# Earlier splits of the rows of O^T and another order of the additions and weights between attention and the feed-forward part of a two-layer trunk

## The chip, the cores and the metric

The kernel runs on one core of one Trainium2 chip. The metric is device time in microseconds (us) of one execution. PE is TensorE, DVE VectorE, ACT ScalarE, POOL GpSimd, and SP SyncE, which issues nearly all DMAs here.

## What is computed

```python
def reference(x, mem, ...):                      # x is 1024 tokens x 1024, two layers
    h = x
    for layer in range(2):
        xn, mn = rmsnorm(h, norm_mix[layer]), rmsnorm(mem, norm_mem[layer])
        proj = xn @ (w_in_fox if layer == 0 else w_in_dil)[0]
        mix = fox_attention(...) if layer == 0 else dilated_attention(...)   # 12 heads of 64
        heads = concat([mix, memory_attention(qm, mn, w_mem_kv[layer])])     # 4 more heads
        h = h + merge_heads(heads) @ w_out[layer]
        h = h + conv_ffn(rmsnorm(h, norm_ffn[layer]), w_up[layer], ...)
    return rmsnorm(h, norm_final)
```

## The kernel before

All values are held transposed, features on partitions and tokens along the free dimension, and the 1024 tokens are worked on as two halves of 512. A float32 product is made of three matmuls: each operand is split into a high part, which is a cast, and a low part, which is the operand less its high part. So a group for one block of 128 input features is high by high (L175), high weights by low input (L176) and low weights by high input (L177). `load_w` fetches a piece of weights of 128x512 by a DMA on SP (L121, four buffers `wraw`), casts it on ACT (L122, `whi`) and subtracts on POOL (L123, `wlo`). A pair `whi`, `wlo` holds two pieces, 128x1024, the weights of one output row, and there are three such pairs.

**Attention.** There are six pairs of heads (`pair` 0 to 5), and in each two heads with eight blocks of queries. `fill` holds generators of matmuls, the projections of the next pairs among them, which are mixed with the blocks' scores (L514, L515), transposes (L531) and products with v (L851) at due times given as numbers (L799 to L808). The softmax of a block runs on DVE (maximum L518, scaling L525) and ACT (exponential L522). Each transposed block is cast on ACT (L532, `pth`) and subtracted on DVE (L533, `ptl`). A projection of k is cast on ACT (L492), subtracted on POOL (L494, `kla`, `klb`) and then moved to other partitions by DMAs on SP (L103). The order on PE follows the program. ACT, DVE, POOL and SP take their instructions in the order that the framework's scheduler makes of it.

**Rows of O^T.** The output of each pair of heads is a row of O^T, 128 features by 1024 tokens. Two more rows come from the memory heads. All rows but that of the last pair are written to DRAM (`o_scr`, L547) and read back, one half at a time, by `load_o`: a DMA on SP (L296), a cast on ACT (L297, `xh`) and a subtraction on POOL (L298, `xl`). The raw row lies in a ring of five buffers (`sqt`), which other short-lived tiles share. The order of the rows (`KORD`) is 0, 1, 2, 3, 6, 7, 4, 5. Row 5 never leaves the chip (`fold`, L543). The tiles `xh` and `xl` of a half are those that held the input of the projections of that half.

**Output projection.** It has eight rows of outputs. `out_part(0, 6)` and `out_part(1, 4)` are generators in `fill` (L807, L808) that multiply the first seven rows of O^T with six rows of outputs of half 0 and four of half 1. Each loads its seven rows of O^T at its start (L604). What is left is done by `out_rest` (L309): the rest of a row that `out_part` began (kind "f", one group, weights `wol`) and whole rows (kind "c", eight groups). Behind each row come the residual's addition on DVE (L302), a store (L329), a square on ACT (L331) and the addition of the square to `acc` on DVE (L333). For half 0 this runs at the end of attention (`out_last`). For half 1 it is `rest_1` (L1066), with the order c4, f0, f1, c5, f2, f3, c6, c7.

**Start of the feed-forward part.** From L1076 on the order on PE, ACT, DVE and POOL is that of the code. `next(rest_1)` issues one row of the above, and `x0` prepares the first three inputs of the up-projection from half 0. The up-projection of a pair of feature blocks `j` takes seven products (`product(j, m, bank)`, four groups each) of sums of weights and sums of inputs. The sums of weights are made by `w_alpha` (an addition on DVE, L944, into a tile `asum`), `w_beta` (none) and `w_delta` (two subtractions, L958). Each is split by a cast on ACT (L972) and a subtraction on POOL (L975). `norm_stages` sums the squares of half 1 over features with matmuls (L136), takes the inverse root on POOL (L140), spreads it on DVE (L142), and broadcasts it by a matmul (L146) when it is next resumed. From the broadcast `rb` the inputs of half 1 are scaled on DVE (L378), cast (L371) and subtracted (L374). product(0,5) is the first one to use them.

## Time and profile before

| what | value |
|---|---|
| median of 3 runs | 2610.03 us (2608.42 to 2611.66) |
| the profiled execution | 2601.88 us, of which the span is 2600.1 us |
| mean granted clock of TensorE in it | 0.983 of full |
| PE busy | 2433.2 us (94%) |
| DVE busy | 1585.9 us (61%) |
| POOL busy | 1244.7 us (48%) |
| ACT busy | 1211.6 us (47%) |

The profile comes from one execution, on a time axis that starts with the span. Busy time is that of instructions on an engine, and issue of DMAs is not counted in it. Matmuls overlap their neighbours, so a busy PE isn't PE at its peak: what is to be read are the stretches in which it idles, the instruction that ended each, and the clock that was granted.

### The profile page before, as it was taken

To read this page: it belongs to the slowest core of one execution; us is meant where nothing else is said; L and a number is where in the kernel's file an instruction comes from. 1 tells how busy PE (TensorE), PEld (TensorE's weight loads), DVE (VectorE), ACT (ScalarE), POOL (GpSimd) and SP (SyncE) were. 2 spreads that over 40 slices of the span, in tenths; PEclk is the share of its full clock that TensorE was granted. 3 is DMA by queue.
4 is the path that set the end of the run, shared out by engine and by line. 5 is a ranking of instruction groups with operands and counts; after the bars stand their busy time and mean duration, and the time that the engine had idled before them with its cause. 6 is when DMAs were issued, how large, how long until landed. Compare 5 with 4: busy or idle time off the path is not lost.

```text
span 2600.1 us, 34495 instructions
## 1 busy us (share of the span) xinstructions
PE 2433.2 (94%) x12274; PEld 2023.5 (78%) x12274; DVE 1585.9 (61%) x2777; ACT 1211.6 (47%) x2192; POOL 1244.7 (48%) x797
## 2 busy tenths in 40 slices
PE   5899999898899999999998899988889999999997
PEld 5778888676688888888877797876767888887886
DVE  6667677667866666523156767675777666665322
ACT  6555555543444443533345555555434434444321
POOL 4332323354566666556453333335436666664543
PEclk9999999999999999999999999999999999999999
DMA  5122222441322222654332222234412222237432
GB/s 175 50 76 58 74 60 88 140 155 52 106 73 93 78 89 90 228 180 145 117 124 60 72 57 68 57 100 152 142 61 81 90 81 73 95 125 237 133 128 77
DMA packets 143829, 269.06 MB, mean 103 GB/s; under 512 B 18716, under 2 KB 23452, under 8 KB 143656
## 3 DMA queue, kind: packets, MB, share of 16 engines
q1 hardware_dynamic: 142792, 266.16, 31.7%
q8 instruction: 96, 1.57, 0.3%
q10 hardware_dynamic: 864, 0.69, 0.1%
q14 instruction: 77, 0.63, 0.1%
HBM read 198.58 MB, written 47.24 MB: 95 GB/s over the span
## 4 chain that ended last, share of the span: by engine, by line
PE 72%; DVE 9%; issue 8%; POOL 4%; ACT 4%; DMA 3%; SPq 0%; POOLq 0%; DVEq 0%; ACTq 0%
PE PS L175 16%; PE PS L176 16%; PE PS L177 16%; PE PS L851 3%; PE PS L531 3%; PE PS L1358 3%; PE PS L1359 3%; PE PS L1360 3%; POOL wlo L123 2%; PE PS L1312 2%; PE PS L1310 2%; PE PS L1311 2%; DVE y L525 1%; DMA graw<-gscr 1%; PE PS L515 1%
## 5 line engine op out<-in xcount | busy, mean ns | idle before, releaser
L123 POOL TENSOR_TENSOR wlo<-wraw,whi 128x512 fp32r<-128x512 f32 x354 | 466.6, 1339 | 621.9 <-ACT whi L122 506.5
L175 PE MATMUL PS<-t,ahi 128*128 128x512 f32 x1056 | 413.8, 392 | 7.5 <-DVE cv L1034 6.7
L176 PE MATMUL PS<-t,ahi 128*128 128x512 f32 x1056 | 413.6, 392 | 4.8 <-DVE t L374 4.8
L177 PE MATMUL PS<-t,alo 128*128 128x512 f32 x1056 | 412.6, 391 | 0.0
L175 PE MATMUL PS<-xh,whi 128*128 128x512 f32 x704 | 307.8, 437 | 24.4 <-ACT whi L122 10.4
L122 ACT CAST whi<-wraw 128x512 fp32r<-128x512 f32 x354 | 201.4, 607 | 242.7 <-issue 67.8
L176 PE MATMUL PS<-xl,whi 128*128 128x512 f32 x704 | 284.5, 404 | 13.2 <-POOL xl L298 13.2
L177 PE MATMUL PS<-xh,wlo 128*128 128x512 f32 x704 | 284.3, 404 | 6.9 <-POOL wlo L123 6.8
L1030 ACT ACTIVATE cv<-PS,cw 128x1024 f32<-128x1024 f32 x88 | 106.2, 1207 | 322.0 <-DVE PS L1011 315.2
L175 PEld LDWEIGHTS PS<-t,ahi 128*128 128x128 f32 x1056 | 198.7, 188 | 54.0 <-issue 9.3
L176 PEld LDWEIGHTS PS<-t,ahi 128*128 128x128 f32 x1056 | 198.6, 188 | 49.3 <-DVE t L374 7.0
L177 PEld LDWEIGHTS PS<-t,alo 128*128 128x128 f32 x1056 | 198.6, 188 | 41.8
L1034 DVE SCALAR_TENSOR_TENSOR cv<-PS,cw,cv 128x1023 f32<-128x1023 f32 (+1 forms) x176 | 221.7, 1278 | 7.4 <-ACT cv L1030 4.3
L975 POOL TENSOR_TENSOR alo<-araw,ahi 128x1024 fp32r<-128x1024 f32 x88 | 212.2, 2413 | 4.4 <-ACT ahi L972 4.4
L522 ACT ACTIVATE y<-y,m 128x128 f32<-128x128 f32 (+1 forms) x192 | 149.2, 778 | 122.4 <-DVE m L518 120.1
L533 DVE TENSOR_TENSOR ptl<-PS,pth 128x512 fp32r<-128x512 f32 (+3 forms) x288 | 152.0, 551 | 56.9 <-ACT pth L532 55.7
L532 ACT CAST pth<-PS 128x512 fp32r<-128x512 f32 (+3 forms) x288 | 129.8, 478 | 101.8 <-PE PS L531 97.9
L175 PEld LDWEIGHTS PS<-xh,whi 128*128 128x128 f32 x704 | 138.4, 197 | 46.3 <-ACT whi L122 13.2
L177 PEld LDWEIGHTS PS<-xh,wlo 128*128 128x128 f32 x704 | 136.4, 194 | 40.7 <-POOL wlo L123 11.1
L176 PEld LDWEIGHTS PS<-xl,whi 128*128 128x128 f32 x704 | 137.7, 196 | 37.0 <-POOL xl L298 21.4
L302 DVE TENSOR_TENSOR h<-h,PS 128x512 f32<-128x512 f32 x56 | 37.7, 685 | 203.3 <-PE PS L1360 165.3
L1281 DVE TENSOR_TENSOR g<-graw,g 128x512 fp32r<-128x512 f32 x88 | 80.2, 942 | 118.8 <-ACT g L1280 118.5
(218 smaller groups left out, 5815.6 us busy)
## 6 DMA issues: line engine op xcount, KB each, us to landing
araw<-in_wu SPq DMA_DIRECT2D x176, 256.0 KB, 3.6
wraw<-in_wd SPq DMA_DIRECT2D x168, 256.0 KB, 3.0
gscr<-cv SPq DMA_DIRECT2D x44, 512.0 KB, 2.6
graw<-gscr SPq DMA_DIRECT2D x88, 256.0 KB, 3.7
wraw<-in_wo SPq DMA_DIRECT2D x64, 256.0 KB, 2.8
wraw<-in_wq SPq DMA_DIRECT2D x56, 256.0 KB, 2.9
hfscr<-h SPq DMA_DIRECT2D x32, 256.0 KB, 2.1
h<-hfscr SPq DMA_DIRECT2D x32, 256.0 KB, 4.0
```

The costliest lines, as they stand in the source:

```text
L122: nc.scalar.copy(hi[:, w], raw[:, :n])
L123: nc.gpsimd.tensor_tensor(lo[:, w], raw[:, :n], hi[:, w].bitcast(F32), op=ALU.subtract)
L175: nc.tensor.matmul(ps, lhsT=whi(k), rhs=xhi(k), start=(first and k == 0), stop=False)
L176: nc.tensor.matmul(ps, lhsT=whi(k), rhs=xlo(k), start=False, stop=False)
L177: nc.tensor.matmul(ps, lhsT=wlo(k), rhs=xhi(k), start=False, stop=(last and k == nk - 1))
L522: nc.scalar.activation(y[:, :nk], y[:, :nk], AF.Exp, bias=m[:, npc - 1:npc], scale=-1.0, accum_out=m[:, 2:3])
L532: nc.scalar.copy(ph, tp[:, :nj, :])
L533: nc.vector.tensor_tensor(pl, tp[:, :nj, :], ph.bitcast(F32), op=ALU.subtract)
L975: eng.tensor_tensor(o[2], o[0], o[1].bitcast(F32), op=ALU.subtract)
L1030: nc.scalar.activation(t, u, AF.Identity, bias=w(3), scale=w(2))
L1034: V.scalar_tensor_tensor(t[:, d:], u[:, :T - d], w(2 - d), t[:, d:], op0=ALU.mult, op1=ALU.add)
L1281: nc.vector.tensor_tensor(t[:, 1, :], raw, t[:, 0, :].bitcast(F32), op=ALU.subtract)
```

## The change

It has four pieces. `load_o` can now load some of its rows and go on later, and six rows of half 0 are loaded by a new generator `o_first`, which stands in `fill` ahead of the last projection of k for half 1 (`pair_k(5, 1)`) and behind that for half 0. The seventh row, row 4, is still loaded at the start of `out_part(0, 6)`. Six rows of half 1 are loaded when `out_part(0, 6)` comes to its third row of outputs. `out_rest` loads the weights of the second whole row before its first row, and those of whole row m+2 behind the matmuls of whole row m, which held the same buffers. At the start of the feed-forward part, residual and square additions of `rest_1` go ahead of `w_alpha(1)` and `w_delta(1)`, `asum` of j = 1 lies in another ring, and the norm's first stage and its broadcast each stand one product later.

```diff
@@ -286,16 +286,20 @@
     def load_h(l, n, half, dst=None):
         nc.sync.dma_start((dst or H[half])(n), a["xT"][:, n, half * HT:half * HT + HT] if l == 0 else h_scr[n][half])
 
-    def load_o(l, half):
-
-        if (l, half) in O:
-            return O[l, half]
-        oh, ol = O[l, half] = x_tiles(half)
-        for c in KORD[:-1]:
+    DONE = {}
+
+    def load_o(l, half, n=NPAIR + 1):
+
+        if (l, half) not in O:
+            O[l, half] = x_tiles(half)
+            DONE[l, half] = 0
+        oh, ol = O[l, half]
+        for c in KORD[DONE[l, half]:n]:
             raw = sqt("oraw")
             nc.sync.dma_start(raw, o_scr[l][c][:, half * HT:half * HT + HT])
             nc.scalar.copy(oh[:, c, :], raw)
             nc.gpsimd.tensor_tensor(ol[:, c, :], raw, oh[:, c, :].bitcast(F32), op=ALU.subtract)
+        DONE[l, half] = max(n, DONE[l, half])
         return oh, ol
 
     def residual(ps, n, half, src=None):
@@ -313,18 +317,19 @@
         whole = [n for kind, n in order if kind == "c"]
         ws = {whole[0]: load_w(a["wo"][l, whole[0]])}
         wl = load_w(a["wol"][l])
+        ws[whole[1]] = load_w(a["wo"][l, whole[1]])
         yield
         for i, (kind, n) in enumerate(order):
             if kind == "f":
                 hi, lo, ks = *wl, [(NPAIR - 1, n)]
             else:
-                m = whole.index(n) + 1
-                if m < len(whole):
-                    ws[whole[m]] = load_w(a["wo"][l, whole[m]])
                 hi, lo, ks = *ws.pop(n), [(c, c) for c in KORD]
             ps = psum()
             mm3(ps, lambda k: cols(hi)(ks[k][1]), lambda k: cols(lo)(ks[k][1]),
                 lambda k: oh[:, ks[k][0], :], lambda k: ol[:, ks[k][0], :], len(ks))
+            m = whole.index(n) + 2 if kind == "c" else len(whole)
+            if m < len(whole):
+                ws[whole[m]] = load_w(a["wo"][l, whole[m]])
             residual(ps, n, half, PART[l] if half and kind == "f" else None)
             nc.sync.dma_start(hf_scr[l][n][half], H[half](n))
             sq = acc if i == 0 else sqt("sq")
@@ -611,11 +616,17 @@
                 for n in range(rows if half else KD):
                     load_h(l, n, half, dst)
                 for n in range(rows):
+                    if half == 0 and n == 2:
+                        load_o(l, 1, NPAIR)
                     hi, lo = load_w(a["wo"][l, n])
                     ps = psp()
                     yield from mm3g(ps, lambda k: cols(hi)(KORD[k]), lambda k: cols(lo)(KORD[k]),
                                     lambda k: oh[:, KORD[k], :], lambda k: ol[:, KORD[k], :], KD - 1, 216)
                     nc.vector.tensor_tensor(dst(n), dst(n), ps, op=ALU.add)
+
+            def o_first():
+                load_o(l, 0, NPAIR)
+                yield 0
 
 
             def out_last():
@@ -801,6 +812,8 @@
                 if v:
                     fill.add(v[0], V, 16 * p - 6, 16 * p - 13, ("va", p))
                 fill.add(pair_k(p, 0), QK, 16 * p - (1.5, 2.5)[l], 16 * p - 8, ("a", p))
+                if p == NPAIR - 1:
+                    fill.add(o_first(), 0, 16 * p - (1.5, 2.5)[l], 16 * p - 8)
                 fill.add(pair_k(p, 1), QK, 16 * p + (2.5, 1.5)[l], 16 * p - 8, ("b", p))
                 if v:
                     fill.add(v[1], V, 16 * p + 6, 16 * p - 13, ("vb", p))
@@ -940,7 +953,7 @@
         def w_alpha(j):
 
             r0, r1 = R[j]
-            s = two(yt("asum") if j == 1 else tab("asum"))
+            s = two(qk("asum", F32) if j == 1 else tab("asum"))
             V.tensor_tensor(s, r0, r1, op=ALU.add)
             h, lo = w_set()
             A[j][2], A[j][5] = ((h[:, i, :], lo[:, i, :]) for i in range(2))
@@ -1082,34 +1095,34 @@
                 next(rest_1)
             next(x0)
             next(x0)
+            next(rest_1)
+            next(rest_1)
+            next(rest_1)
             oa = w_alpha(1)
             cast(oa)
+            next(x0)
             next(rest_1)
             rest(oa, G)
-            next(rest_1)
-            next(rest_1)
-            next(x0)
+            run(x0)
             ob = w_beta(1)
             cast(ob)
+            rest(ob, G)
+            next(rest_1)
+            run(rest_1)
             od = w_delta(1)
-            run(x0)
-            next(rest_1)
-            rest(ob, G)
-            cast(od)
-            next(rest_1)
-            rest(od, G)
-            run(rest_1)
             product(0, 2, 6)
             s_copy(0, 2)
+            product(1, 2, 2)
             st = norm_stages(acc, lambda: bank_of("norm", (7, 5)))
             next(st)
-            product(1, 2, 2)
             s_copy(1, 2)
+            cast(od)
+            rest(od, G)
             product(0, 4, 0)
+            product(1, 4, 4)
             rb = next(st)
             prep(0, (w_gamma,), G)
             prep(1, (w_gamma,), G)
-            product(1, 4, 4)
             u21(0)
             for c in range(2):
                 norm_in_place(l, 1, rb, (4 + 2 * c, 5 + 2 * c))
```

ACT in layer 1, around the last projection of k (`roper` and `ropeq` belong to it; `y` is a block of the softmax, `pth` the cast of a transposed block, `xh` that of a row of O^T), before:

```order
L522 ACTIVATE y,m<-y,m 128x768
L522 ACTIVATE y,m<-y,m 128x896
L540 COPY fold<-PS 64x512
L492 CAST ka<-ropeq 64x512
L532 CAST pth<-PS 128x4x128
L492 CAST kb<-ropeq 64x512
L532 CAST pth<-PS 128x128
L532 CAST pth<-PS 128x4x128
L522 ACTIVATE y,m<-y,m 128x1024
L532 CAST pth<-PS 128x2x128
L522 ACTIVATE y,m<-y,m 128x128
```

and after:

```order
L300 CAST xh_15382<-oraw 128x512
L497 CAST ka<-ropeq 64x512
L300 CAST xh_15382<-oraw 128x512
L497 CAST kb<-ropeq 64x512
L300 CAST xh_15382<-oraw 128x512 x2
L537 CAST pth<-PS 128x4x128
L527 ACTIVATE y,m<-y,m 128x1024
L537 CAST pth<-PS 128x128
L537 CAST pth<-PS 128x4x128
L545 COPY fold<-PS 64x512
L537 CAST pth<-PS 128x2x128
L300 CAST xh_15382<-oraw 128x512 x2
```

Four of the six casts of rows of half 0 now stand ahead of the 1024-wide exponential, one of them ahead of the casts of k (`ka`, `kb`) and one between these, and two stand behind it. In layer 0 all six stand ahead of it.

ACT in layer 0 at the start of the feed-forward part (`whi` are weights of whole rows, `h` and `sq` the rows and squares of `out_rest`, `t` an input and `asum`, `araw` weights of the up-projection), before:

```order
L371 CAST t_5881<-h_4937 128x1024 x2
L122 CAST whi<-wraw 128x512 x2
L331 ACTIVATE acc<-h_5871 128x512
L331 ACTIVATE sq<-h_5870 128x512 x2
L371 CAST t_5950<-tsum 128x1024
L972 CAST ahi<-asum 128x1024
L122 CAST whi<-wraw 128x512 x2
L331 ACTIVATE sq<-h_5871 128x512
L331 ACTIVATE sq<-h_5870 128x512 x2
L371 CAST t_5950<-tsum 128x1024
```

and after:

```order
L376 CAST t_5891<-h_4937 128x1024 x2
L122 CAST whi<-wraw 128x512 x2
L336 ACTIVATE acc<-h_5881 128x512
L336 ACTIVATE sq<-h_5880 128x512 x2
L376 CAST t_5960<-tsum 128x1024
L122 CAST whi<-wraw 128x512 x2
L336 ACTIVATE sq<-h_5881 128x512
L336 ACTIVATE sq<-h_5880 128x512 x2
L985 CAST ahi<-asum 128x1024
L376 CAST t_5960<-tsum 128x1024
```

Before, the two casts of weights here are those of the second whole row and, behind the cast of `asum`, those of the third. Now the second row's come earlier than this piece, and those of the third and of the fourth both stand ahead of `asum`.

PE in layer 0 around the broadcast of the norm of half 1 (`t` with its number is the input of a product), before, where it stands between product(0,4) and product(1,4):

```order
L175 MATMUL PS<-t_5950,ahi 128x512
L176 MATMUL PS<-t_5950,ahi 128x512
L177 MATMUL PS<-t_5950,alo 128x512
L146 MATMUL PS<-dg,ones 128x512
L175 MATMUL PS<-t_5950,ahi 128x512
L176 MATMUL PS<-t_5950,ahi 128x512
L177 MATMUL PS<-t_5950,alo 128x512
```

and after, where it stands between product(1,4) and product(0,5):

```order
L175 MATMUL PS<-t_5960,ahi 128x512
L176 MATMUL PS<-t_5960,ahi 128x512
L177 MATMUL PS<-t_5960,alo 128x512
L146 MATMUL PS<-dg,ones 128x512
L175 MATMUL PS<-t_6175,ahi 128x512
L176 MATMUL PS<-t_6175,ahi 128x512
L177 MATMUL PS<-t_6175,alo 128x512
```

The broadcast moved behind twelve matmuls; L136 moved in the same way behind product(1,2).

## Rows read from the trace of the kernel before

**Rows 1.** the page's chain that ended last, share of the span by engine

```profile
PE 72%; DVE 9%; issue 8%; POOL 4%; ACT 4%; DMA 3%; SPq 0%; POOLq 0%; DVEq 0%; ACTq 0%
```

**Rows 2.** PE's waits, 440 to 620 us: total us, times, longest us

```profile
PE PS L175 <- ACT xh L297: 6.3, 2, 5.3
...
PE PS L175 <- ACT whi L122: 4.0, 3, 3.1
```

**Rows 3.** timeline of ACT: start us, us, instruction, count [idle before <-releaser]

```profile
466.74 0.86 ACT L532 CAST pth<-PS 128x512 fp32r<-128x512 f32 x2 [1.73 <-PE PS L531]
```

**Rows 4.** timeline of PE around the start of layer 0's output projection

```profile
477.16 0.23 PE L517 MATMUL PS<-trim,identb 128*128 128x128 bf16 x1
482.69 0.79 PE L175 MATMUL PS<-xh,whi 128*128 128x512 f32 x1 [5.29 <-ACT xh L297]
...
492.57 0.27 PE L515 MATMUL PS<-kla,qa 128*128 128x128 f32 x1
```

**Rows 5.** stretches: us, busy PE, PEld, DVE, ACT, POOL, PEclk, DMA, GB/s

```profile
482.20:492.40 10.20, 7.58 (x16) 4.68 (x17) 0.59 (x2) 4.31 (x8) 6.88 (x6) 0.50 1.00 321
...
605.10:611.90 6.80, 6.07 (x13) 4.30 (x14) 3.65 (x6) 2.75 (x6) 5.74 (x3) 0.50 0.30 116
```

**Rows 6.** SP's timeline, layer 0, and DMA issues (count, KB, us to landing)

```profile
480.77 0.50 SPq L103 DMA_DIRECT2D kla<-kla  x1
...
kla<-kla SPq DMA_DIRECT2D x24, 128.0 KB, 2.2
```

**Rows 7.** instructions on the raw rows: ns min/median/max; then their DMAs

```profile
L297 ACT CAST xh<-oraw x28: 602/619/622, 482.0 to 1813.5; 128x512 fp32r<-128x512 f32 x28
L298 POOL TENSOR_TENSOR xl<-oraw,xh x28: 1256/1276/1537, 482.8 to 1818.4; 128x512 fp32r<-128x512 f32 x28
...
DMA to landing us min/median/max: 2.6/4.2/5.1
```

**Rows 8.** timelines of PE and of SP, the same place in layer 1

```profile
1767.55 0.27 PE L515 MATMUL PS<-kla,qa 128*128 128x128 f32 x1
...
1758.41 0.50 SPq L103 DMA_DIRECT2D kla<-kla  x1
```

**Rows 9.** SP's timeline in layer 0, the move for half 0

```profile
461.27 0.48 SPq L103 DMA_DIRECT2D kla<-kla  x1
```

**Rows 10.** PE's waits, 493 to 560 us, then 1800 to 1830 us

```profile
PE PS L176 <- POOL xl L298: 4.1, 5, 1.5
...
PE PS L176 <- POOL xl L298: 4.3, 6, 1.3
```

**Rows 11.** PE's timeline, layer 0, the last 26 groups of the output projection

```profile
593.57 0.39 PE L177 MATMUL PS<-xh,wlo 128*128 128x512 f32 x1
...
620.90 0.39 PE L177 MATMUL PS<-xh,wlo 128*128 128x512 f32 x1
...
621.58 0.39 PE L177 MATMUL PS<-xh,wlo 128*128 128x512 f32 x1
```

**Rows 12.** ACT's timeline in the same stretch

```profile
604.08 1.04 ACT L972 CAST ahi<-asum 128x1024 fp32r<-128x1024 f32 x1 [2.66 <-DVE asum L944]
605.03 1.13 ACT L122 CAST whi<-wraw 128x512 fp32r<-128x512 f32 x2
```

**Rows 13.** PE's waits, 1870 to 1900 us

```profile
PE PS L175 <- ACT whi L122: 4.6, 3, 3.0
```

**Rows 14.** PE's timeline, layer 0, the broadcast and the start of product(0,5)

```profile
630.93 1.02 PE L146 MATMUL PS<-dg,ones 128*128 128x512 f32 x2
...
634.56 0.48 PE L175 MATMUL PS<-t,ahi 128*128 128x512 f32 x1
```

**Rows 15.** line L525, all its instructions; then timelines of POOL and DVE

```profile
L525 DVE TENSOR_SCALAR y<-y,m x192: 285/625/1506, 167.7 to 1838.8; 128x128 f32<-128x128 f32 x24, 128x256 f32<-128x256 f32 x24, 128x384 f32<-128x384 f32 x24, 128x512 f32<-128x512 f32 x24
...
475.42 2.52 POOL L123 TENSOR_TENSOR wlo<-wraw,whi 128x512 fp32r<-128x512 f32 x2 [12.80 <-ACT whi L122]
...
476.65 1.51 DVE L525 TENSOR_SCALAR y<-y,m 128x384 f32<-128x384 f32 x1
```

## The prediction, made before the changed kernel had run

> **What bounds the kernel now.** I read the page's chain of work first: TensorE (PE) holds 72% of the chain and no other engine over 9% [rows 1]. The question of any change here is therefore which idle stretches of PE it fills. The table of PE's waits over the end of layer 0's attention and its output projection (440 to 620 us) names them: 6.3 us for the cast `xh` of a row of O^T (L297), and 4.0 us for a cast of weights `whi` (L122), of which one wait is 3.1 [rows 2]. These are the things the change moves. Layer 1 has the same places with like sizes, so each term below is worked out in layer 0 and then set against layer 1. The profiled execution took 2601.9 us (span 2600.1), 8.1 us under the median of the three runs, 2610.0; I make the sum in the profiled execution's microseconds and take it off the median, since a difference of 0.3% between the two scales moves a sum of 28 us by 0.1.
>
> **Part A, half 0's rows of O^T one projection earlier.** In layer 0 PE ends the scores of a block at 477.16, then has nothing until 482.69, where the first matmul of the output projection waits 5.29 us for the cast of its row; it reaches the next block's 128x128 scores (L515) at 492.57 [rows 4]. In between it ran at a granted clock of 0.50, that is 1.2 GHz, after the idle of 5.29 [rows 5]. With rows already split, the work in between is four groups of three matmuls (0.68 each, see C) and under a microsecond of others, so PE would arrive at the L515 by 481. It can't go on then: those scores read the low half of k of the last projection, whose move is issued at 480.77 and takes 2.2 us to land [rows 6], thus until 483.0. What is late next is this move. The gain without any side effect is 492.57 - 483.0 = 9.5 us. In layer 1 the same matmul comes at 1767.55, and the move is issued at 1758.41 [rows 8], landing at 1760.6: 6.9 us. So 16.4 us is the upper bound of A.
>
> The price is on ScalarE. Six casts of 0.62 us (L297) and on GpSimd six subtractions of 1.28 us [rows 7] now stand between the exponentials of the last head pair's blocks, in program order (the listing of ScalarE above). Before, ScalarE sat idle 1.73 us before the softmax's cast at 466.74 and the 1024-wide exponential followed it [rows 3]. Now that exponential stands behind the sixth cast. On SyncE's queue four of the six rows go behind the moves of k for half 0, of which `kla` went at 461.27 [rows 9]; with two moves and four rows of about 0.5 us of issue behind it, the sixth goes at 464.5 and lands 4.2 us later [rows 7], at 468.7, its cast done at 469.3 to 470. The exponential was due at 467.6: 1.8 to 2.6 us late, taken as 2.6 because PE's transposes wait for it. Such a wait may bring the low clock on PE for a stretch (below), for which I charge 1.5. Layer 0 then gives 9.5 - 2.6 - 1.5 = 5.4. In layer 1 four of the six casts stand in front of the 1024-wide exponential, between the two casts of k, so that k's own move waits for landings; four casts are 2.5 us, and half of a landing of 4.2 is uncovered, 2.4 with the gap: 4.9. With 1.0 for the clock, 6.9 - 4.9 - 1.0 = 1.0. A gives **6.4 us**, between -6.9 (each layer pays two whole landings and all six casts, 2 x 4.2 + 3.7, less the 1.7 of idle, 10.4; 16.4 - 20.8 - 2.5 for the clock) and 16.4. I take a value near the middle because the trace shows the casts' durations and landings, but not how the order on ScalarE and SyncE lets them collide.
>
> **Part B, half 1's rows behind the third row of half 0's projection.** Before, the first groups of half 1's projection wait for the subtraction `xl` five times in layer 0, 4.1 us, and six times in layer 1, 4.3 us [rows 10]. PE uses the rows faster (0.68 a group) than GpSimd makes them (1.28 each). Issued four projection rows earlier they are done: six subtractions are 7.7 us on GpSimd, in front of the third row's weights, while one projection row on PE is seven groups of 0.68 and attention between. So B is worth 4.1 + 4.3 = **8.4 us**; if the weights of row three come late instead, 5.
>
> **Part C, weights and additions of the rest of half 1.** From the group that ends with the matmul at 593.57 to the one at 621.58 PE runs 26 groups of three matmuls in 28.0 us [rows 11]. A group at full clock takes 0.68 us (the spacing of the last groups, 621.58 less 620.90), so 26 take 17.7. The difference, **10.3 us**, is one chain: the weights of the third whole row are cast only at 605.03, because they stand on ScalarE behind the cast of `asum`, which itself waited 2.66 us for VectorE's addition [rows 12]; PE waits 3.1 us for them [rows 2] and runs the next stretch at a clock of 0.50 [rows 5], and the fourth row's come late the same way. After the change the second row's weights are there before the first yield, those of the third go out when the first row's matmuls end, about 592, and must be there at 593.8 + 10 x 0.68 = 600.6; cast and subtraction of two halves take about 5 us. That they fit is the reason to take the whole 10.3. Covers that go: GpSimd's subtraction of `beta` and `delta` of the first up-projection now stands behind the second row's weights, but their products come only after 611. Layer 1 runs the same 26 groups with waits for weights of 4.6 us in place of 4.0 [rows 13], so I count 10.3 again: **20.6 us**.
>
> **Part D, the norm's broadcast behind one more product.** The ones-matmuls (L136) move behind product(1,2) and cost nothing. The broadcast (L146) moves behind product(1,4). From it to product(0,5) it is 634.56 - 630.93 = 3.63 us [rows 14]: VectorE's four scalings, a cast and a subtraction, a chain that the change leaves as long as it was. Before, the twelve matmuls of product(1,4), 4 x 0.68 = 2.7 us, ran inside it. Now they run ahead, and PE idles instead: 2.7 us a layer, **-5.4 us**. The idle adds to a PE wait just behind it, and idles of 3.1 and 5.29 us were each followed by a granted clock of 0.50 for 6.8 and 10.2 us [rows 5]. I charge 1.0 a layer, -2.0, from 0 to 3.4 (half of 6.8, if all of such a stretch came back).
>
> **The sum.** 6.4 + 8.4 + 20.6 - 5.4 - 2.0 = 28.0. The profiled execution would take 2573.9, the median 2610.0 - 28.0 = **2582.0 us**.
>
> **A rule of the skill.** In the trace a scaling of VectorE (L525) of 384 columns took 1.51 us where the median of all its widths is 0.625 [rows 15]; GpSimd was subtracting weights at that time, two pieces in 2.52 us [rows 15]. The Trainium skill, "SBUF — State Buffer", section "Who interferes with whom", says that VectorE and GpSimd share a pair of ports, that the one that issues first holds it for its whole instruction, and that a tensor_scalar can be of the kind that needs it. The long row agrees with that. It speaks against Part A, which puts six GpSimd subtractions among these scalings: that is the third rival.
>
> **The rivals.**
> 1. ScalarE gives the gain of A back: the casts wait for landings in front of exponentials, and A is at its low end, -6.9 in place of 6.4. Then 28.0 - 13.3 = 14.7: 2595.3 us. For it: ScalarE takes its work in order, and a landing is 4.2 us. Against: it is busy 47% of the span (the table of the profile).
> 2. Everything hides: A 16.4, no clock charge. 16.4 + 8.4 + 20.6 - 5.4 = 40.0: 2570.0 us, and lower by what restarts after eleven waits cost. For it: the casts are short. Against: the order puts the sixth cast before the exponential.
> 3. VectorE's scalings beside GpSimd's subtractions: about four in each layer take 0.9 us longer (1.51 - 0.625), in the softmax's chain that PE waits for: 8 x 0.9 = 7.2, so 20.8 is left: 2589.2 us.
> 4. The weights of the third and fourth row are still late, since GpSimd has six more halves to subtract and `beta`, `delta` between; half of C goes: 17.7 is left, 2592.3 us.
> 5. **Slower.** The place is the ring of row buffers in Part A. If only one is free, each row waits for the one before: landing 4.2, cast 0.62, subtraction 1.28 [rows 7], 6.1 us a row and 36.6 for six. Begun at 461.3 [rows 9] they end at 497.9, and the exponential behind them, due at 467.6, with it. From there PE has 13.2 us to go to the marker (477.4 - 467.6, and 3.4 of the work above), which it reaches at 511.1 instead of 492.57: 18.5 us late in each layer. The other parts give 8.4 + 20.6 - 7.4 = 21.6, so the kernel takes 2610.0 - 21.6 + 37.0 = 2625.4 us. It decides from a loss of 10.8 us a layer, that is from 4.8 us a row. Against it: the ring has five buffers.
>
> **How the numbers follow.** About 0.2%, 5 us, is what a measurement of this kernel can tell from no change. Chances: the forecast 0.46 (2573 to 2589 with its terms' bounds), rival 1 0.15, rival 2 0.13, rival 3 0.09, rival 4 0.05, rival 5 0.06; that losses of several rivals add up to within 0.2% has 0.06. The first five are faster by over 0.2%: 0.88. The range reaches from 2567 (rival 2 with restarts) to 2598 (rival 1 with the bounds of B); it leaves out rival 5 and the case of no change.
>
> **What would show it.** In the changed kernel's trace: no wait of PE for row casts or row subtractions at either layer's output projection (A, B); PE's next 128x128 L515 reached about 483 by the old scale, or ScalarE's 1024-wide exponential late behind row casts (rival 1); 26 groups in about 17.7 us with a clock of 1.00 before the first product (C); an idle of PE of about 2.7 us right behind the moved broadcast, in front of product(0,5), and its clock behind it (D). L525 rows above 1 us beside GpSimd would show rival 3. The prediction is wrong if PE's waits move into the transposes of the last head pair (L531's successor waiting for VectorE's `ptl`), or if the 26 groups still hold waits for weights.

## The result, and the profile after

The median of four runs was 2582.25 us (2581.41 to 2587.91), against 2610.85 of four runs of the kernel before (2608.42 to 2612.58). The ratio is 0.9898, 95% interval 0.9884 to 0.9912. That is 28.6 us less where 28.0 were forecast. Of the four terms inside the sum only one came out as closely, as the stretches below show.

The page of the changed kernel (busy us and share; then the chain) reads much like the one before, PE 94% busy and 72% of the chain. A change of 1% doesn't show at this level:

```profile
PE 2426.6 (94%) x12274; PEld 2026.8 (79%) x12274; DVE 1600.9 (62%) x2777; ACT 1211.3 (47%) x2192; POOL 1247.5 (48%) x797
...
PE 72%; DVE 10%; issue 7%; ACT 4%; DMA 3%; POOL 3%; SPq 1%; POOLq 0%; DVEq 0%; ACTq 0%
```

PE's waits over 440 to 600 us of the changed kernel (total, times, longest) answer to [rows 2] and [rows 10]. The waits for `xh`, `whi` and GpSimd's `xl` are gone. Other ones have come, for the move of k (`ka`) and, in front of the products with v (L864), for `ptl` and `pth`, the split of transposed blocks; the wait of the transposes (L536) for `ptl` was there before too, and has grown. (Lines up to L288 keep their numbers; those behind are up to 13 higher in the changed kernel, and shifted a little more in some experiments, so L515 is L520, L531 is L536, L522 is L527, L297 is L300, L374 is L379.)

Before (440 to 620 us), then the changed kernel:

```profile
PE PS L531 <- DVE ptl L533: 2.7, 3, 1.6
```

```profile
PE PS L519 <- DMA ka<-ka: 3.6, 1, 3.6
PE PS L536 <- DVE ptl L538: 3.4, 3, 2.2
PE PS L864 <- DVE ptl L538: 1.5, 2, 1.0
PE PS L864 <- ACT pth L537: 1.0, 1, 1.0
```

For each part there is a stretch between two matmuls that both kernels have, in the same order. Its length in each trace is worked out from PE's timeline as the difference of two start times (us).

| part and stretch | layer | before | after | moved by | forecast |
|---|---|---|---|---|---|
| A: 128x128 scores two blocks ahead of the last projection's half 1, to those of the second head | 0 | 69.74 | 67.39 | -2.4 | -5.4 |
| | 1 | 71.27 | 68.91 | -2.4 | -1.0 |
| B: from the next 128x128 scores, some 21 us on, to the first wait for `wlo` behind them | 0 | 28.01 | 22.49 | -5.5 | -4.1 |
| | 1 | 28.05 | 22.20 | -5.9 | -4.3 |
| C: the last 26 groups of the output projection | 0 | 28.01 | 17.69 | -10.3 | -10.3 |
| | 1 | 28.01 | 17.68 | -10.3 | -10.3 |
| D: first product to the first with the `adia` weights | 0 | 29.50 | 35.22 | +5.7 | +3.7 |
| | 1 | 29.46 | 33.62 | +4.2 | +3.7 |

These sum to -26.8 before rounding. The rest of the program is not the same in two executions of even the same kernel, as the next section shows.

**C** went as forecast, in both layers. Where [rows 11] had 28.0 us, the first and last of its three rows are now 17.69 apart, at a clock of 1.00, and no wait of PE lies between them (timeline of PE, then the stretch with busy us of PE, PEld, DVE, ACT, POOL, clock, DMA, GB/s):

```profile
589.01 0.39 PE L177 MATMUL PS<-xh,wlo 128*128 128x512 f32 x1
...
606.70 0.39 PE L177 MATMUL PS<-xh,wlo 128*128 128x512 f32 x1
```

```profile
589.00:607.00 18.00, 18.00 (x81) 14.90 (x80) 17.86 (x22) 9.74 (x16) 8.45 (x5) 1.00 0.28 104
```

**D** cost more. PE's timeline behind the first products shows the forecast idle in front of product(0,5), 2.58 us where 2.7 was said, and one that was not forecast, 1.14 us ahead of the ones-matmuls (L136), for the last addition to `acc`. Both idles are there in layer 1 too. The clock fell behind a different one in each layer (second fence): in layer 0 behind the ones-matmuls, 0.70 over the 5.7 us there, and it was 1.00 behind product(0,5); in layer 1 behind product(0,5), 0.54 over 6 us. At that pace PE waits 0.61 us where it waits 0.88 in layer 0, and not at all where it waits 0.78, 0.38 and 0.76, so the stretch of layer 1 is the shorter one.

```profile
613.66 1.15 PE L136 MATMUL PS<-ones,acc 128*128 128x1 f32 x8 [1.14 <-DVE acc L341]
...
625.31 0.50 PE L175 MATMUL PS<-t,ahi 128*128 128x512 f32 x1 [2.58 <-ACT t L376]
```

```profile
612.30:618.00 5.70, 4.57 (x17) 3.66 (x17) 4.39 (x6) 2.59 (x4) 2.91 (x2) 0.70 0.12 46
...
1889.00:1895.00 6.00, 6.00 (x15) 4.70 (x16) 5.97 (x8) 1.05 (x1) 0.00 (x0) 0.54 0.00 0
```

### The profile page after: what moved, and what is told of

The parts are those of the page before. It is cut to its first block, busy times and chain, and to the rows that moved or that the text cites. A ratio compares the mean times of both kernels' runs of the same rounds, so it can differ in the third digit from the quotient of the medians.

```text
span 2579.6 us, 34484 instructions
## 1 busy us (share of the span) xinstructions
PE 2426.6 (94%) x12274; PEld 2026.8 (79%) x12274; DVE 1600.9 (62%) x2777; ACT 1211.3 (47%) x2192; POOL 1247.5 (48%) x797
## 4 chain that ended last, share of the span: by engine, by line
PE 72%; DVE 10%; issue 7%; ACT 4%; DMA 3%; POOL 3%; SPq 1%; POOLq 0%; DVEq 0%; ACTq 0%
PE PS L175 16%; PE PS L176 16%; PE PS L177 16%; PE PS L864 3%; PE PS L536 3%; PE PS L1371 3%; PE PS L1373 3%; PE PS L1372 3%; PE PS L1325 2%; PE PS L1324 2%; PE PS L1323 2%; POOL wlo L123 2%; DMA graw<-gscr 1%; DVE y L530 1%; PE PS L520 1%
## 5 line engine op out<-in xcount | busy, mean ns | idle before, releaser
L527 ACT ACTIVATE y<-y,m 128x128 f32<-128x128 f32 (+1 forms) x192 | 149.3, 778 | 123.1 <-DVE m L523 121.2
L536 PE MATMUL PS<-ident,y 128*128 128x128 f32 x864 | 129.3, 277 | 26.4 <-DVE ptl L538 26.3
```

The lines of the kernel that those rows point to most:

```text
L527: nc.scalar.activation(y[:, :nk], y[:, :nk], AF.Exp, bias=m[:, npc - 1:npc], scale=-1.0, accum_out=m[:, 2:3])
L536: nc.tensor.transpose(tp[:, jj, :], y[:, j * P:(j + 1) * P], ident)
```

## The experiments

**The kernel before, profiled again.**

> The kernel before once more, for a second profile of it. If a profile repeats within 0.3%, PE reaches the first matmul behind the k move of layer 0 within 1 us of 492.57 and the span is 2600; if single profiles scatter as widely as the timed runs (2605 to 2616), the stretches show where the scatter sits, and terms read from one profile of each are uncertain by as much.

It took 2612.8 us with a span of 2611.0, 11 us more than the first profile. The stretches of the table repeat to 0.3 us in these two (69.74 and 70.06, 71.27 and 71.06, 29.50 and 29.45, 29.46 and 29.53). In all traces that have them, the changed B and C repeat to 0.1 us; A and D do not. With A in the program, five traces (`after`, `a_only`, `rb_early`, `port_off`, `port_rb`) have 66.95 to 70.63 us for A in layer 0 and 67.05 to 69.99 in layer 1; without it, four have 69.74 to 71.69 and 71.06 to 71.33. The means differ by 2.4 and 2.2 us, so that the 4.7 us which the table gives A holds, though a single pair of traces could have shown much less or more. Most of the 11 us are four steps elsewhere: 2.4 us by 70 us from the start, 2.9 around 1110, 3.1 between 1935 and 1980, 1.2 around 2385. In the third the granted clock was lower, as the same 165 matmuls show in the first profile and in this one, where they come 6.6 us later:

```profile
1935.00:1980.00 45.00, 39.04 (x165) 30.90 (x165) 40.15 (x43) 20.30 (x22) 21.31 (x10) 0.99 0.34 117
```

```profile
1941.60:1989.70 48.10, 43.73 (x165) 34.08 (x165) 40.17 (x44) 21.82 (x24) 22.35 (x11) 0.88 0.32 110
```

The spans of single profiles can thus differ by about 10 us for such steps alone. The medians of the kernel before, from five sets of timed runs, lie between 2610.85 and 2612.61 us.

**Each part alone.** `a_only` is the kernel before with the changed `load_o` and this generator; `b_only` with the changed `load_o` and these two lines; `cd_only` is the changed kernel without both.

```diff
 # a_only
+                if p == NPAIR - 1:
+                    fill.add(o_first(), 0, 16 * p - (1.5, 2.5)[l], 16 * p - 8)
 # b_only
+                    if half == 0 and n == 2:
+                        load_o(l, 1, NPAIR)
```

> Only Part A: six rows of half 0 split ahead of the last projection of k, all else as before. By the stretches of PE in the two traces (layer 0 from 2.4 us behind to level at the first matmuls behind the k move, layer 1 by 2.6) A is worth about 5 us: 2606. The prediction's term of 6.4 says 2604.5. If ScalarE gives back what the rows save (rival 1, -6.9) it is 2617.8. If this is only part of a gain that needs B, nothing: 2610.9.

> Only Part B: six rows of half 1 split from the third row of half 0's projection on. In the changed kernel's trace the eleven waits are gone and PE is ahead by 5.4 and 5.1 us over these stretches: 10.5, that is 2600.4. The prediction's term of 8.4 (idle alone) says 2602.5. If the third row's weights come late for it, 5: 2605.9.

> Parts C and D without A and B. By the traces the 26 groups give 10.0 and 10.1 us, and the norm's move costs 5.5 and 4.4: 10.2 net, 2600.7. The prediction's terms are 20.6 - 7.4 = 13.2: 2597.7. If C and D need the earlier rows to be worth anything, under 5.

| run | median us | ratio to before | 95% interval |
|---|---|---|---|
| a_only | 2607.3 | 0.9989 | 0.9977 to 1.0000 |
| b_only | 2600.8 | 0.9962 | 0.9949 to 0.9976 |
| cd_only | 2599.7 | 0.9957 | 0.9941 to 0.9973 |

The three are worth 2.9, 9.9 and 11.2 us by their ratios, 24 together against the 26.6 of the whole change by its ratio: they add up, within their intervals. A is the small one, and the interval of its ratio reaches 1.0000. B is over the forecast, and a table of PE's waits between 493 and 560 us of `b_only` has one row left, where [rows 10] had five waits for `xl` of 4.1 us in all (the wait below was in the trace of before too, a little later):

```profile
PE PS L177 <- POOL wlo L123: 0.9, 1, 0.9
```

`cd_only` has C and D together. C's earlier loads of weights and the new place of `w_alpha(1)` both change what stands on ScalarE ahead of these weights, and no run takes the two apart.

**What A loses on.** In `a_noact` the six rows come straight into the tiles by two DMAs each; in `a_nopool` only the low tile is filled so, and ScalarE still casts. Both leave out the subtraction, and the first the cast too: such a tile holds the whole row, unsplit.

```diff
 # a_noact
+            if plain:
+                nc.sync.dma_start(oh[:, c, :].bitcast(F32), o_scr[l][c][:, half * HT:half * HT + HT])
+                nc.sync.dma_start(ol[:, c, :].bitcast(F32), o_scr[l][c][:, half * HT:half * HT + HT])
+                continue
 # a_nopool
             nc.scalar.copy(oh[:, c, :], raw)
+            if plain:
+                nc.sync.dma_start(ol[:, c, :].bitcast(F32), o_scr[l][c][:, half * HT:half * HT + HT])
+                continue
```

> The changed kernel with the six early rows of half 0 fetched straight into the high and the low tiles, 12 DMAs and no casts or subtractions (the low parts are left wrong). If casts waiting for landings on ScalarE ate A's gain (rival 1, half true), the 1024-wide exponential of layer 0 is no longer 2.6 us late, PE's waits for ptl near it fall from 4.7 to 1.6 us, and the kernel gains about 4 us a layer less what 1.5 MB more of DMA cost: 2575. If the move of k is what bounds, PE's waits for ka there stay at 3.6 and 3.1 or grow: 2582 or more.

> The changed kernel with the casts of the six early rows of half 0 left on ScalarE, and GpSimd's subtractions replaced by a second DMA straight into the low tiles (which are left wrong). If ScalarE's order eats A (casts waiting for landings ahead of exponentials), the two attention stretches stay as in the changed kernel, 67.4 and 68.9 us: 2582. If GpSimd's subtractions beside VectorE's scalings do it (rival 3), they fall to the 61.3 and 65.2 us of the run without either: 2572.

`a_noact` took 2570.5 us (ratio 0.9835, 0.9822 to 0.9849), `a_nopool` 2582.6 (0.9888, 0.9871 to 0.9905). The A stretches are 61.25 and 65.15 us in the first, 67.93 and 69.88 in the second; in the changed kernel they were 67.39 and 68.91. So the rows' way through ScalarE and GpSimd costs 10 of the 14.6 us that splitting them early would be worth. The timeline of ScalarE shows one part of how, the exponential in the trace of before and then the changed kernel:

```profile
467.73 1.15 ACT L522 ACTIVATE y<-y,m 128x1024 f32<-128x1024 f32 x1
```

```profile
469.03 1.38 ACT L300 CAST xh<-oraw 128x512 fp32r<-128x512 f32 x2 [0.49 <-DMA oraw<-oscr]
470.32 0.58 ACT L537 CAST pth<-PS 128x512 fp32r<-128x512 f32 x1
471.59 1.27 ACT L300 CAST xh<-oraw 128x512 fp32r<-128x512 f32 x2 [0.69 <-DMA oraw<-oscr]
472.76 1.15 ACT L527 ACTIVATE y<-y,m 128x1024 f32<-128x1024 f32 x1
```

This trace runs 2.38 us behind the one before at 444.73 (442.35 there), so the 1024-wide exponential stands 2.65 us later than the 467.73 that it had. In `a_noact`, 0.77 behind, it is at its old place:

```profile
468.49 1.15 ACT L531 ACTIVATE y<-y,m 128x1024 f32<-128x1024 f32 x1
```

In `a_nopool` the scheduler gave ScalarE another order: three casts stand behind that exponential, and behind the first of them the copy of `fold`, which stands ahead of the exponential in the traces of before, of the changed kernel and of `a_noact`. The addition on VectorE that follows this copy frees the bank that PE's next products with v write; PE waits 3.45 us for it (timelines of ScalarE, VectorE and PE):

```profile
472.26 0.75 DVE L533 TENSOR_SCALAR y<-y,m 128x1024 f32<-128x1024 f32 x1
...
472.44 0.62 ACT L300 CAST xh<-oraw 128x512 fp32r<-128x512 f32 x1 [0.41 <-DMA oraw<-oscr]
...
473.48 0.58 ACT L548 COPY fold<-PS 64x512 f32<-64x512 f32 x1
...
474.84 0.57 PE L867 MATMUL PS<-pth,vt 128*128 128x256 f32 x1 [3.45 <-DVE fold L549]
```

So casts alone, in that order, cost as much as casts and subtractions do in the changed kernel. That does not clear GpSimd's subtractions, since the order changed when they went. The scaling of 1024 columns takes 0.75 us here and 1.12 in the changed kernel, where a subtraction runs beside it. Another one there, of 896 columns, takes 1.69 us, where it took 0.69 in the trace of before, and right behind it stands PE's longest wait for `ptl` in this stretch (VectorE before; then VectorE, GpSimd and PE of the changed kernel):

```profile
463.86 0.69 DVE L525 TENSOR_SCALAR y<-y,m 128x896 f32<-128x896 f32 x1
```

```profile
466.72 1.69 DVE L530 TENSOR_SCALAR y<-y,m 128x896 f32<-128x896 f32 x1
...
465.06 2.87 POOL L301 TENSOR_TENSOR xl<-oraw,xh 128x512 fp32r<-128x512 f32 x2
...
469.07 0.87 PE L536 MATMUL PS<-ident,y 128*128 128x128 f32 x6 [2.23 <-DVE ptl L538]
```

This is the sign by which rival 3 was to show. How the 10 us part between the casts and the subtractions is left open. In layer 1 the transposes' wait for `ptl` over the A stretch grew too, before and after:

```profile
PE PS L531 <- DVE ptl L533: 2.0, 2, 1.6
```

```profile
PE PS L536 <- DVE ptl L538: 4.6, 3, 3.4
```

What is late next is the move of k, as forecast, but later than forecast: the whole chain to it shifts with the exponential, and `ka` lands 4.3 us after its issue. In the trace of before the move of `kla` at this place had already taken 3.8 us (first fence), and not the 2.2 that is the median of all 24. PE's row at the first 128x128 scores that need the move, in the changed kernel and in `a_noact`:

```profile
DMA to landing us min/median/max: 3.8/3.8/3.8
```

```profile
490.77 0.30 PE L519 MATMUL PS<-ka,qa 128*128 128x128 f32 x1 [3.65 <-DMA ka<-ka]
```

```profile
483.71 0.30 PE L523 MATMUL PS<-ka,qa 128*128 128x128 f32 x1 [2.06 <-DMA ka<-ka]
```

**D's broadcast.** `rb_early` puts the broadcast back ahead of product(1,4).

```diff
             product(0, 4, 0)
+            rb = next(st)
             product(1, 4, 4)
-            rb = next(st)
```

> The changed kernel with the broadcast back ahead of product(1,4); the ones-matmuls stay behind product(1,2). If the cost of D is cover taken from the chain behind the broadcast, the 2.58 us idle in front of product(0,5) goes to under 0.5 in each layer and the kernel takes 2582.3 - 5 = 2577. If that chain is late for another reason (the squares' sum, VectorE's order), PE waits as long for the broadcast's operand instead and it stays at 2582.

It took 2583.1 us (ratio 0.9898, 0.9884 to 0.9913): no change. In the trace the wait in front of product(0,5) fell from 2.58 to 0.31 us, but the D stretch only from 35.22 to 33.02 (layer 1: 33.62 to 33.00), and in layer 1 PE waits 1.35 us for the broadcast's operand instead. That is the other half of what was expected: VectorE makes this operand (`dg`) in 2.86 us in layer 1, where in the trace of before it took 0.69 us in layer 0 (timelines of VectorE, before and then `rb_early`):

```profile
626.81 0.69 DVE L142 TENSOR_TENSOR dg<-ident,nrs 128x512 f32<-128x512 f32 x1 [1.12 <-POOL nrs L140]
```

```profile
1883.68 2.86 DVE L142 TENSOR_TENSOR dg<-ident,nrs 128x512 f32<-128x512 f32 x1 [1.12 <-POOL nrs L140]
```

In the changed kernel `dg` and two more rows are as long. Its VectorE and GpSimd, in the D stretch of layer 0:

```profile
605.75 2.48 DVE L338 TENSOR_TENSOR acc<-acc,sq 128x512 f32<-128x512 f32 x1
608.15 3.41 DVE L379 TENSOR_TENSOR t<-tsum,t 128x1024 fp32r<-128x1024 f32 x1
...
616.13 2.87 DVE L142 TENSOR_TENSOR dg<-ident,nrs 128x512 f32<-128x512 f32 x1 [1.12 <-POOL nrs L140]
```

```profile
605.26 2.42 POOL L988 TENSOR_TENSOR alo<-asum,ahi 128x1024 fp32r<-128x1024 f32 x1 [4.05 <-ACT ahi L985]
607.86 2.62 POOL L988 TENSOR_TENSOR alo<-araw,ahi 128x1024 fp32r<-128x1024 f32 x1 [0.19 <-ACT ahi L985]
...
616.07 2.39 POOL L988 TENSOR_TENSOR alo<-araw,ahi 128x1024 fp32r<-128x1024 f32 x1
```

Each long row of VectorE ends 0.5 to 1.1 us after a subtraction on GpSimd that began before it: 608.23 after 607.68, 611.56 after 610.48, 619.00 after 618.46. `port_off` gives the subtractions of `alpha` and `beta` to VectorE and has GpSimd do that of `delta` later; `port_rb` is that with the early broadcast.

```diff
-            rest(oa, G)
+            rest(oa, V)
             run(x0)
             ob = w_beta(1)
             cast(ob)
-            rest(ob, G)
             next(rest_1)
             run(rest_1)
+            rest(ob, V)
             od = w_delta(1)
...
             cast(od)
-            rest(od, G)
...
             prep(1, (w_gamma,), G)
+            rest(od, G)
```

> The changed kernel with the split subtractions of alpha and beta (j = 1) on VectorE instead of GpSimd, that of beta behind the last squares, and GpSimd's of delta behind those of gamma; PE's order stays. If VectorE's long additions (acc 2.48, t 3.41, dg 2.87 where 0.68, 1.22 and 0.69 are their usual durations) are blocked by GpSimd's subtractions beside them, they fall to the usual ones, the 1.14 us wait for acc and the 0.50 clock behind it go, some 3 us a layer: 2576. If those durations are VectorE's own there, it has 2.4 us more work a layer and acc comes later: 2585.

> As port_off, and the broadcast ahead of product(1,4). If D's cost is cover lost, and the broadcast's operand was late only for GpSimd, both the 1.14 us wait and the 2.58 us idle go and PE reaches product(0,5) some 5 us earlier in each layer: 2571 to 2573. If the chain behind the broadcast is late for another reason, as port_off.

`port_off` took 2579.9 us (ratio 0.9882, 0.9867 to 0.9897), `port_rb` 2580.2 (0.9877, 0.9863 to 0.9890). VectorE's rows in `port_off` have their usual length, although it now has the two subtractions to do as well:

```profile
605.58 0.68 DVE L338 TENSOR_TENSOR acc<-acc,sq 128x512 f32<-128x512 f32 x1
606.18 1.21 DVE L988 TENSOR_TENSOR alo<-asum,ahi 128x1024 fp32r<-128x1024 f32 x1
607.31 1.21 DVE L379 TENSOR_TENSOR t<-tsum,t 128x1024 fp32r<-128x1024 f32 x1
...
614.47 0.69 DVE L142 TENSOR_TENSOR dg<-ident,nrs 128x512 f32<-128x512 f32 x1 [1.12 <-POOL nrs L140]
```

The wait for `acc` is gone, and the D stretch is 32.21 and 32.25 us; in `port_rb` it is 31.32 and 31.31. So without GpSimd beside VectorE the D stretch is 3.0 us shorter in layer 0 and 1.4 in layer 1, and the broadcast's place gives 0.9 more in each. (In traces with D's order as in the changed kernel the stretch is 33.6 to 35.3 us in either layer, so 1.4 to 3 is the size of the first term.) In `port_rb` the delayed subtraction of `delta` (GpSimd, 616.67, 2.38 us) meets the next long operation of VectorE, which takes 3.00 where 1.22 is usual, and PE waits 2.65 us for it: part of the cost has only moved.

```profile
617.13 3.00 DVE L379 TENSOR_TENSOR t<-h,t 128x1024 fp32r<-128x1024 f32 x1
...
620.19 0.50 PE L176 MATMUL PS<-t,ahi 128*128 128x512 f32 x1 [2.65 <-DVE t L379]
```

Against the changed kernel the stretches give 4.4 and 6.2 us. The timed runs show 2 us by the medians, 4 and 5 by the ratios, whose intervals overlap with that of the changed kernel, so that as times these two gains aren't settled.

**Splitting the rows where they are made.** `fold_split` casts and subtracts each of the six rows of half 0 when its heads are folded and stores both parts; `best` adds `port_rb`; `best_l0` is `best` with the condition `l == 0` added, so that layer 1 loads its rows as the changed kernel does. The rows are then fetched as in `a_noact`, from the two stored parts.

```diff
+                if half == 0 and c in KORD[:NPAIR]:
+                    hi = sqt("fhi").bitcast(R32)
+                    nc.scalar.copy(hi[rows, :], t[rows, :])
+                    nc.vector.tensor_tensor(t[rows, :].bitcast(R32), t[rows, :], hi[rows, :].bitcast(F32), op=ALU.subtract)
+                    move(ohi_scr[l][c][rows, :], hi[rows, :])
                 nc.sync.dma_start(o_scr[l][c][rows, half * HT:half * HT + HT], t[rows, :])
```

> The changed kernel with the split of the six early rows of half 0 done where each row is folded, on ScalarE (64x512, 0.62 us) and VectorE (0.68 us), twelve of each in a layer spread over the whole of attention, and both parts written to DRAM and fetched by two plain DMAs. If what A lost is the bunch of casts and subtractions in one projection, the two stretches fall to 61 and 65 us and nothing else grows: 2572. If attention has no slack on ScalarE and VectorE elsewhere, the 24 pieces, 15.6 us a layer, show as waits of PE for pth and ptl: 2582 or more.

> fold_split and port_rb together. If the terms add, 8 to 10 us off for the rows and 2 to 8 for the first products: 2565 to 2572. If the time is set by stretches at the low clock that come behind short idles at random, it stays within a few us of the better of the two, 2572.

> As best, with the rows split at their folds in layer 0 alone; layer 1 loads and splits them as the changed kernel does. In fold_split layer 0's attention before the last pair grew by 2 us and the last stretch fell by 5 to 6, and layer 1's attention grew by 11. If these terms hold, 3 to 4 us for the rows and 2 to 8 for the first products: 2570 to 2577. If the low-clock stretches decide, 2580 as port_rb and best.

`fold_split` took 2585.1 us (ratio 0.9899, 0.9884 to 0.9915). Its A stretches fell to 61.90 and 66.93, the 61 that was expected in layer 0, but in layer 1 the attention ahead of them (from its first scores at 1410 us to 1718) grew from 298.2 us in the changed kernel and 297.2 in `a_nopool` to 308.2. PE's waits for `ptl` there are 16.0 us, and ones for the rotated q and k on ScalarE (`roper`) have come; in the changed kernel (1407.5 to 1705.7 us) the first were 12.6:

```profile
PE PS L541 <- DVE ptl L543: 16.0, 13, 2.8
PE PS L524 <- ACT roper L473: 2.7, 2, 1.8
```

```profile
PE PS L536 <- DVE ptl L538: 12.6, 10, 2.4
```

In layer 0 the same stretch grew by 2 us. So the pieces find more room in layer 0 than in layer 1, and `best` stayed at 2580.3 (0.9887, 0.9870 to 0.9903). `best_l0` took 2576.8 us, ratio 0.9865 (0.9848 to 0.9881), an interval below that of the changed kernel (0.9884 to 0.9912): it is faster than the changed kernel too. Its A stretches are 60.33 and 66.93 us, its D stretches 31.54 and 31.28.

## Why the prediction was right, point by point

The reading that the idle of PE around the output projections is what can be won, and that it is on the path, held: in B and C the waits are gone and the stretches run at the pace that nothing holds up, and the whole program is shorter by about the sum of the four parts.

**A** (forecast 6.4, measured 4.7 by the stretches, 2.9 by `a_only`). The mechanism held: rival 1 in part, with the 1024-wide exponential 2.65 us late in layer 0. The 2.6 of the prediction is close to that by a slip, since its own times, 469.3 to 470 against 467.6, make 1.7 to 2.4. The term was mis-sized on two counts. In layer 0 I charged that delay once, and PE paid more: waits for `ptl` and `pth` beyond the delay, and a move of k that lands 4 us after its issue where I took 2.2, the median of 24 moves, although this very move took 3.8 in the trace that I read. In layer 1 I charged too much, 4.9 us. A sign that I had named for being wrong, waits in the transposes for `ptl`, came in part: from 2.0 to 4.6 us in layer 1. Rival 3, GpSimd's subtractions beside the softmax's scalings, came in part as well, 1.69 us in place of 0.69 for one scaling; no run gives its price apart from that of the casts. Rival 5, one row at a time, did not come about. What the upper bound was worth is shown by `a_noact`: 14.6 of the 16.4 us are there when no engine has to handle the rows.

**B** (forecast 8.4, measured 11.4). The step that failed was counting the idle alone. PE's timeline of before shows three matmuls, the second of which waits:

```profile
534.60 0.40 PE L175 MATMUL PS<-xh,whi 128*128 128x512 f32 x1
535.45 0.51 PE L176 MATMUL PS<-xl,whi 128*128 128x512 f32 x1 [0.46 <-POOL xl L298]
535.79 0.39 PE L177 MATMUL PS<-xh,wlo 128*128 128x512 f32 x1
```

Where nothing waits such rows start 0.23 us apart, each before the one ahead has ended. Here the starts are 0.85 and 0.34 apart: 0.73 us are lost where the row shows 0.46. The missing overlap ahead of the waiting matmul is 0.16 of the difference, the later start of the one behind it 0.11. Eleven waits at 0.27 us each make the 3 us by which B was too small; the range of 5 to 8.4 was on the wrong side.

**C** (forecast 20.6, measured 20.7). The pace of the groups, times their count, was enough, and rival 4, weights still late, did not come about.

**D** (forecast 7.4, measured 9.9). The idle in front of product(0,5) was 2.58 us as forecast. The step that failed is "the ones-matmuls cost nothing": `acc` is late, and with it L136 by 1.14 us, for a clash that the reading of ScalarE's and PE's orders couldn't show. With the weights early, GpSimd's subtractions for the up-projection fall on the last squares, and `port_off` shows that VectorE's additions are three to four times as long for it. The Trainium skill, "SBUF — State Buffer", section "Who interferes with whom", says that a VectorE instruction with two inputs in SBUF contends with a GpSimd instruction that reads SBUF, and that the one that issues later is blocked until the other is done. This trace agrees: the 2.48, 3.41 and 2.87 us in place of 0.68, 1.21 and 0.69. I had thought of such a clash for the scalings in the softmax alone, and not for these two-input additions. The clock's charge of 1.0 us a layer came, but not at one place: in layer 0 behind the ones-matmuls, in layer 1 behind product(0,5). That the cost of D lies in cover taken away, as I argued, is shown for 0.9 us a layer, and `port_rb`, which gives that number, has a new wait of 2.65 us in it.

**The sum.** Over A and D I was 4 us too optimistic, over B 3 us too pessimistic. Of the 28.6 us between the medians 26.8 lie in the stretches; the remaining 2 are no more than what the low-clock stretches elsewhere change from one execution to the next. So the near agreement of 28.0 and 28.6 is in part luck. I also set the profiled execution's scale equal to that of the median. The first profile of before was a quick one: with it the two spans differ by 20.5 us only, with the second by 31.4.

## What to carry to other kernels

Work that is moved ahead still goes through an engine that takes its queue in order. Ask for each of its pieces which DMA it waits for and what stands behind it; the rows that `a_noact` kept off ScalarE and GpSimd gained three times as much as the same rows split there. Count a wait as the gaps around the waiting matmul less their usual spacing, not as the idle that its row shows. Take the landing of a transfer from the row of that transfer, not from a median of quieter places. When a change fills an idle stretch, look at which engines' long operations now fall side by side: here GpSimd's subtractions beside VectorE's additions cost 1.4 to 3 us a layer.

## What the runs showed of the hardware that was not expected

Stretches of PE at the lower clock come behind short idles, most of them of 1 to 4 us, at many places, and not at the same ones in each execution of one kernel; in the changed kernel's trace the 1.14 us ahead of the ones-matmuls brought one in layer 0 and none in layer 1. The matmuls of 512 columns whose rows are 0.6 us or longer, in place of 0.39, cover 67 us in the first profile of before and 81 in the second, 58 in the changed kernel and 72 in `port_rb`. At half the clock, the 14 us between the two profiles of one kernel are some 7 us of time, an estimate that makes up most of the 11 by which they differ. What decides at which idle the clock falls is left open.
